# The pooling layer's input product over both column halves at once, and the memory's product in small banks

## The chip, the core and the metric

The kernel runs on one core of a Trainium2 chip. The metric is the device time of one execution in microseconds; three runs of the kernel before are given.

## What is computed

Two decoder layers, on 256 tokens of 1024 features, in float32. Layer 0 matters here:

```python
h = rms_norm(x, g_mix[0]) @ w_in_pool[0]           # 1024 x 1024
tok = pool_mixer(h[..., :768], w_pool_group, pool_scale)   # trailing means - itself, times 4 groups of 192 x 192
qm = h[..., 768:]                                   # 256 columns: 4 heads of 64
mo = mem_cross_attention(qm, rms_norm(mem, g_mem[0]), w_mem_kv[0], ...)   # keys and values: 1024 x 512
x = x + concatenate([tok, mo]) @ w_out[0]
x = x + square(relu(rms_norm(x, g_mlp[0]) @ w_ff1[0])) @ w_ff2[0]
```

Layer 1 has causal attention in place of pooling, the same memory attention with its own weights, and another MLP.

## The kernel before, in words

Every product of float32 matrices is done in three terms. A helper makes two halves of a number: `split` (L105) and `evac_split` (L122) write a high half on the scalar engine (ACT; L113, L125, L128) and a low half on the vector engine (DVE; L114, L126, L129), and `mm3` (L117) issues three matmuls: high by high, high by low, low by high (L118 to L120). Weights come from HBM into slots of `rawp` (7 slots of 512 KB, tag "raw"), all on the queue of the sync engine (SP).

PSUM's eight banks are two pools of four: `accp` for accumulators of products (`accum`, L75) and `psp` for everything that is short (`psum`, L72): transposes, bands, groups, scores.

The input product of layer 0 is x^T (8 chunks of 128 features, two blocks of 128 tokens) by 1024 columns of weights. It runs in two passes over all features: the *B half* (columns 512 to 1023, accumulators `aB`) with loads of x and of the weights in turns (L491 to L512), and then the *A half* (columns 0 to 511, `aA`, L534) by `in_chunk` (L194), which loads two chunks of features in one transfer. Within the A half, hooks issue other work before a given chunk: `queries` before chunk 5 (copies, squares and transposes of the memory's queries, L530), `load_x` before 6 (rows of x for the norms, L526), `load_bands` before 7 (L520).

Then `mix_stats` (L470) forms the norms of x, with a power on POOL (L163); the transposed memory is loaded and split (`mth`, `mtl`); the pooled channels are emptied with the norm (`hhi`, `hlo`). `mem_kv_mm` (L223) makes keys and values of the memory, for layer 0 in `aK` (L616), with the hook `pooling` (L592) before chunk 5: it empties `aA`, loads the group weights, and does four pairs of band products (L563) and three pairs of group products (L580). `mem_kv_norm` and `mem_kv_finish` (L226, L234) read `aK`. The second layer's memory product (`aK1`, L634) follows, with the steps of the memory attention as hooks, and then the output projection, which takes four accumulators.

The program text is not the final order. A planner (the Tile framework's scheduler) gives each engine and each queue a fixed order: among the instructions that its own costs say are ready, the one that stands first in the program goes first. On the chip an engine keeps to that order and waits.

What the change touches, in code:

```python
        hooks = [(PLAN['x'], load_x), (PLAN['q'], queries), (PLAN['bw'], load_bands)]
        aA = in_chunk(xT, w_in_pool[0], 0, GMIX, hooks=hooks)
...
        aK = mem_kv_mm(0, [(PLAN['pool'], pooling)])
```

Of the kernel before, what the change touches and what calls it, by code (L numbers as in the profile page):

```python
# [10 lines left out]
F32 = mybir.dt.float32  # L11
# [7 lines left out]
P = 128  # L19
# [10 lines left out]
# columns of the packed small inputs  # L30
# [6 lines left out]
LAG = 2  # L37
# chunk of features of an input product before which other work is issued (8: after the last), and orders of issue
PLAN = {'x': 6, 'q': 5, 'bw': 7, 'pool': 5, 'mem0': (1, 3, 6, 6),
# [3 lines left out]
B0 = P + 16  # tokens that the first block reaches  # L43

# pairs (input chunk, output chunk) of 128 pooled channels that share a group of 192
# [8 lines left out]
def trunk(ctx: ExitStack, tc: tile.TileContext, x, mem, x_t, mem_t, small, bands, rope, mask,  # L54
# [29 lines left out]
    # the tensor engine's clock rises only under load, and the activation tables load on first use  # L84
# [10 lines left out]
    def load_raw(src):  # L95
        """src: rows (k 128) by n columns, k * n = 1024 -> tile [P, k, n]."""
        n = src.shape[1]
        k = src.shape[0] // P
        r = rawp.tile([P, k, n], F32, tag="raw", name=nm("raw"))
        nc.sync.dma_start(r, src.rearrange("(k p) n -> p k n", p=P))  # L100
        return r
# [20 lines left out]
    def evac_split(ps, hi, lo, g=None):  # L122
        """hi + lo = ps (times the per-partition g)."""
# [7 lines left out]
    def transpose4(src, ncol, hi, lo):  # L131
        """src [P tokens, ncol*128] -> hi/lo [P, ncol, 128 tokens]."""
# [12 lines left out]
    def residual_t(b, h, t):  # L145
        """columns of half h of block b of the residual -> transposed halves."""
# [3 lines left out]
    def norm_stats(src, name, after=None):  # L150
        """mean(src^2) + EPS over the row, [P, 1]."""
# [29 lines left out]
    def head_r(z, nh, eps64, name, ss=None):  # L181
        """(sum(z^2) + 64 eps ms)^-1/2 per head: 1/8 of the head's normalising factor."""
# [11 lines left out]
    def in_chunk(t, w, c0, gcol, c1=None, hooks=()):  # L194
        """token-major (t^T @ (g w)) for 512 columns from c0 on (or 256 from c0 and 256 from c1) -> two accumulators."""
        a = [accum(), accum()]
# [24 lines left out]
    mkp = ctx.enter_context(tc.tile_pool(name="mkp", bufs=1))  # L221

    def mem_kv_mm(l, hooks=()):  # L223
        return in_chunk(memT, w_mem_kv[l], 0, GMEM + 8 * l, hooks=hooks)
# [9 lines left out]
    def mem_kv_finish(l, a, kn, pool):  # L234
        """the normalised keys, transposed, and the values; the last of three steps returns them."""
# [16 lines left out]
    def mem_q(a, b, qT):  # L252
        """queries [P tokens, 256] in PSUM -> transposed hi/lo, and the sums of squares per head."""
# [10 lines left out]
    # work that follows a batch of scores is issued LAG batches later  # L264
# [11 lines left out]
    def exp_t(pool, entries, p, nbuf, put):  # L276
        """entries: (src, n, scale, nbias); later: transposed probabilities [keys, 128] side by side to put()."""
# [27 lines left out]
    def mem_scores(b, j, mq, mk, a, pool, nbuf, put):  # L305
        """heads j, j + 2 of block b -> p^T [keys, (head, key block) 128 tokens]."""
# [14 lines left out]
    def av_out(cat, c0, srcs):  # L321
        """srcs[h][b]: lists of (p^T, values) of 4 heads -> chunks c0, c0 + 1 of the transposed concatenation."""
# [11 lines left out]
    def mem_heads(cat, mq, mk, a, pool, nbuf):  # L334
        """the steps of the memory attention: the scores of either block, then what gathers them."""
# [130 lines left out]
    # ================= layer 0: pooling mixer =================  # L466
# [9 lines left out]
    with tc.tile_pool(name="l0", bufs=1) as lp:  # L476
# [3 lines left out]
        def split_t(src, k, t):  # L480
            """two chunks of 128 features of a transposed input -> its halves."""
            evac_split(src, t[0][:, k:k + 2, :], t[1][:, k:k + 2, :])
# [6 lines left out]
        # first chunk: the loads of x and of the weights take turns  # L489
        aB = [accum(), accum()]  # L490
        for k in range(0, NKC, 2):  # L491
            if k == 0:
                xt = rawp.tile([P, 2, S], F32, tag="raw", name=nm("raw"))
                raws = []
                for j in range(2):
                    nc.sync.dma_start(xt[:, j, :], x_t[:, j, :])
                    raws.append(load_raw(w_in_pool[0][j * P:(j + 1) * P, 512:1024])[:, 0, :])
                    if j == 0:
                        nc.sync.dma_start(sm[:, :16], small[:, :16])
                    evac_split(xt[:, j, :], xT[0][:, j, :], xT[1][:, j, :])  # L500
            else:
                xt = load_t(x_t, k)
                r = load_raw(w_in_pool[0][k * P:(k + 2) * P, 512:1024])
                raws = [r[:, 0, :], r[:, 1, :]]
                if k == 4:
                    nc.sync.dma_start(sm[:, 16:], small[:, 16:])
                split_t(xt, k, xT)
            for j in range(2):
                p = split(raws[j], sm[:, GMIX + k + j:GMIX + k + j + 1])
                for b in range(2):  # L510
                    mm3(aB[b], blk(xT, b, k + j), p, k + j == 0, k + j == NKC - 1)
# [20 lines left out]

        hooks = [(PLAN['x'], load_x), (PLAN['q'], queries), (PLAN['bw'], load_bands)]
        aA = in_chunk(xT, w_in_pool[0], 0, GMIX, hooks=hooks)  # L534
        after_chunk(hooks)
# [3 lines left out]
        # memory: transposed halves  # L539
# [3 lines left out]
        # pooled channels: token-major halves, trailing means, group products  # L543
# [9 lines left out]
        def band(o, w, n, c):  # L553
            """o[128 channels of chunk c, n windows from w on, 256 tokens]: trailing mean minus the value itself."""
# [302 lines left out]
```

## Time and profile before

| | us |
|---|---|
| median of three runs | 572.84 |
| lowest, highest | 572.65, 574.88 |
| span of the profiled execution | 572.7 |
| TensorE (PE) busy | 563.7 |
| DVE busy | 375.6 |
| ACT busy | 340.9 |
| POOL busy | 24.4 |

The span runs from the first to the last instruction of one profiled execution; its own time is not listed beside it, and the three runs are other executions. Busy times of PE are those of a pipelined engine: a matmul of 512 columns shows 0.39 us, but the next starts 0.23 us later. PEld is the load of the stationary operand. "SPq" is the issue of a transfer on the sync engine's queue. A bracket at the end of a timeline row is the idle time of the engine before it, and what ended it.

### The profile page before, as it was taken

How to read it: one execution, taken by the hardware profiler on the slowest of the kernel's cores; microseconds unless marked ns; L12 is line 12 of the kernel's file. 1: busy time of each engine (PE TensorE's matmuls, PEld its weight loads, DVE VectorE, ACT ScalarE, POOL GpSimd, SP SyncE). 2: the span in 40 equal slices, each digit the busy share in tenths (PEclk: the TensorE clock that was granted, in tenths of full speed). 3: DMA queues.
4: the chain of work that ended last, by engine and by line, in shares of the span. 5: the costliest groups of instructions: out<-in, count | busy, mean ns of one | idle time of the engine just before them, and what ended most of it. 6: DMA issues, size and time to landing. Idle time of an engine off the chain costs nothing.

```text
span 572.7 us, 9233 instructions
## 1 busy us (share of the span) xinstructions
PE 563.7 (98%) x3396; PEld 487.0 (85%) x3396; DVE 375.6 (66%) x737; ACT 340.9 (60%) x635; POOL 24.4 (4%) x27
## 2 busy tenths in 40 slices
PE   7999999999999999999999999999999999999997
PEld 3888778989899898898877777889998988989985
DVE  4798977673764754746879999667647457466342
ACT  5789976563663753745766887657536547356230
POOL 0101210000000000000012112000000000000000
PEclk8999999999999999999999999999999999999999
DMA  7988764644836637448473343454466374484201
GB/s 260 338 287 312 236 191 142 200 157 159 260 122 207 222 117 250 167 132 271 144 216 116 111 137 115 124 176 148 145 225 207 123 259 143 152 264 132 84 0 73
DMA packets 46700, 102.00 MB, mean 178 GB/s; under 512 B 3648, under 2 KB 11584, under 8 KB 46656
## 3 DMA queue, kind: packets, MB, share of 16 engines
q1 hardware_dynamic: 46656, 101.43, 55.1%
q8 instruction: 26, 0.43, 0.3%
q14 instruction: 18, 0.15, 0.1%
HBM read 100.37 MB, written 1.05 MB: 177 GB/s over the span
## 4 chain that ended last, share of the span: by engine, by line
PE 91%; DVE 3%; ACT 2%; DMA 1%; POOL 1%; issue 1%; SPq 0%; DVEq 0%; ACTq 0%
PE acc L119 19%; PE acc L118 19%; PE acc L120 19%; PE step L120 9%; PE step L119 9%; PE step L118 9%; PE av_out L331 1%; DMA raw<-in_w_in_pool_dram 1%; PE exp_t L295 1%; POOL r L163 1%; PE transpose L137 1%; PE tok_scores L707 1%; ACT hi L113 1%; DVE lo L114 1%; PE qk_evac L694 1%
## 5 line engine op out<-in xcount | busy, mean ns | idle before, releaser
L114 DVE SCALAR_TENSOR_TENSOR lo<-raw,sm,hi 128x512 fp32r<-128x512 f32 x212 | 149.8, 748 | 43.1 <-ACT hi L113 42.9
L113 ACT ACTIVATE hi<-raw,sm 128x512 fp32r<-128x512 f32 x212 | 142.0, 716 | 56.5 <-PE acc L120 30.2
L111 DVE TENSOR_TENSOR lo<-raw,hi 128x512 fp32r<-128x512 f32 (+1 forms) x152 | 99.5, 687 | 38.7 <-ACT hi L110 38.3
L110 ACT ACTIVATE hi<-raw 128x512 fp32r<-128x512 f32 (+1 forms) x152 | 91.4, 626 | 52.5 <-PE acc L120 42.5
L120 PE MATMUL acc<-hi,hl 128*128 128x512 f32 x256 | 101.1, 395 | 0.0
L118 PE MATMUL acc<-hi,hh 128*128 128x512 f32 x256 | 101.0, 395 | 0.0
L119 PE MATMUL acc<-lo,hh 128*128 128x512 f32 x256 | 101.0, 395 | 0.0
L119 PE MATMUL step<-x1T,hi 128*128 128x256 f32 x224 | 63.4, 283 | 0.0
L120 PE MATMUL step<-x1T,lo 128*128 128x256 f32 x224 | 63.4, 283 | 0.0
L119 PE MATMUL step<-x3T,hi 128*128 128x256 f32 x224 | 63.4, 283 | 0.0
L120 PE MATMUL step<-x3T,lo 128*128 128x256 f32 x224 | 63.4, 283 | 0.0
L118 PE MATMUL step<-x1T,hi 128*128 128x256 f32 x224 | 63.4, 283 | 0.0
L118 PE MATMUL step<-x3T,hi 128*128 128x256 f32 x224 | 63.4, 283 | 0.0
L397 DVE SCALAR_TENSOR_TENSOR h<-step,r 128x512 f32<-128x512 f32 x28 | 19.3, 689 | 67.1 <-ACT r L394 67.1
L120 PEld LDWEIGHTS acc<-hi,hl 128*128 128x128 f32 x256 | 48.2, 188 | 11.2
L394 ACT ACTIVATE r<-step 128x512 f32<-128x512 f32 x28 | 16.5, 588 | 69.1 <-PE step L120 69.1
L118 PEld LDWEIGHTS acc<-hi,hh 128*128 128x128 f32 x256 | 48.3, 189 | 10.5
L119 PEld LDWEIGHTS acc<-lo,hh 128*128 128x128 f32 x256 | 48.2, 188 | 10.5
L118 PEld LDWEIGHTS step<-x3T,hi 128*128 128x128 f32 x224 | 43.0, 192 | 0.3
L118 PEld LDWEIGHTS step<-x1T,hi 128*128 128x128 f32 x224 | 43.0, 192 | 0.3
L119 PEld LDWEIGHTS step<-x3T,hi 128*128 128x128 f32 x224 | 43.0, 192 | 0.3
L119 PEld LDWEIGHTS step<-x1T,hi 128*128 128x128 f32 x224 | 43.0, 192 | 0.3
(155 smaller groups left out, 948.1 us busy)
## 6 DMA issues: line engine op xcount, KB each, us to landing
raw<-in_w_ff_dram SPq DMA_DIRECT2D x128, 512.0 KB, 4.6
raw<-in_w_out_dram SPq DMA_DIRECT2D x16, 512.0 KB, 4.2
raw<-in_w_in_moba_dram SPq DMA_DIRECT2D x24, 256.0 KB, 4.0
raw<-in_w_mem_kv_dram SPq DMA_DIRECT2D x8, 512.0 KB, 5.3
raw<-in_w_in_moba_dram SPq DMA_DIRECT2D x8, 512.0 KB, 4.6
raw<-in_w_in_pool_dram SPq DMA_DIRECT2D x7, 512.0 KB, 7.2
xr<-in_x_dram SPq DMA_DIRECT2D x2, 512.0 KB, 8.5
raw<-in_mem_t_dram SPq DMA_DIRECT2D x4, 256.0 KB, 6.9
```

The source lines that it names most:

```text
L110: nc.scalar.activation(hi, raw, AF.Copy)
L111: nc.vector.tensor_tensor(lo, raw, hi.bitcast(F32), op=ALU.subtract)
L113: last_hi[0] = nc.scalar.activation(hi, raw, AF.Copy, scale=g)
L114: nc.vector.scalar_tensor_tensor(lo, raw, g, hi.bitcast(F32), op0=ALU.mult, op1=ALU.subtract)
L118: nc.tensor.matmul(o, a[0], b[0], start=start, stop=False)
L119: nc.tensor.matmul(o, a[0], b[1], start=False, stop=False)
L120: nc.tensor.matmul(o, a[1], b[0], start=False, stop=stop)
L137: nc.tensor.transpose(ps[:, c * P:(c + 1) * P], src[:, (c0 + c) * P:(c0 + c + 1) * P], ident)
L163: nc.gpsimd.tensor_tensor(r, src, mhalf[:, :n], op=ALU.pow)
L295: nc.tensor.transpose(ps[:, c * P:(c + 1) * P], p[:, c * P:(c + 1) * P], ident)
L394: nc.scalar.activation(r[:, :n], z, AF.Relu)
L397: nc.vector.scalar_tensor_tensor(h[:, :n], z, 0.0, r[:, :n], op0=ALU.max, op1=ALU.mult)
```

## The change

The pooling layer's input product runs once over the features. For each of the 8 chunks one transfer brings all 1024 columns of weights (rows of 4 KB); the first two chunks' halves come in separate transfers of 256 KB, the B halves first. The first weights and the first gains are issued from ACT's queue. The B half of chunk k is multiplied as it comes, the A half of chunk k - 2 after it (`LAG_A = 2`). All four accumulators are taken at once. `load_x`, `queries` and `load_bands` stand after the loop, between the last A pieces. The memory's product of layer 0 accumulates in two banks of the small pool; that of layer 1 still in accumulators. Three entries of `PLAN` and the comments go.

```diff
-PLAN = {'x': 6, 'q': 5, 'bw': 7, 'pool': 5, 'mem0': (1, 3, 6, 6),
+LAG_A = 2
+PLAN = {'pool': 5, 'mem0': (1, 3, 6, 6),
...
-    def in_chunk(t, w, c0, gcol, c1=None, hooks=()):
-        a = [accum(), accum()]
+    def in_chunk(t, w, c0, gcol, c1=None, hooks=(), a=None):
+        a = [accum(), accum()] if a is None else a
...
-    def mem_kv_mm(l, hooks=()):
-        return in_chunk(memT, w_mem_kv[l], 0, GMEM + 8 * l, hooks=hooks)
+    def mem_kv_mm(l, hooks=(), a=None):
+        return in_chunk(memT, w_mem_kv[l], 0, GMEM + 8 * l, hooks=hooks, a=a)
...
-        aB = [accum(), accum()]
-        for k in range(0, NKC, 2):
-            if k == 0:
+        aB, aA = [accum(), accum()], [accum(), accum()]
+        wraw = {}
+
+        def fetch(k):
+            w = w_in_pool[0]
+            if k < 2:
                 xt = rawp.tile([P, 2, S], F32, tag="raw", name=nm("raw"))
-                raws = []
+                nc.sync.dma_start(xt[:, 0, :], x_t[:, k, :])
+                r = rawp.tile([P, 2, 512], F32, tag="raw", name=nm("raw"))
+                q = nc.scalar if k == 0 else nc.sync
+                q.dma_start(r[:, 1, :], w[k * P:(k + 1) * P, 512:1024])
+                if k == 0:
+                    nc.scalar.dma_start(sm[:, :16], small[:, :16])
+                evac_split(xt[:, 0, :], xT[0][:, k, :], xT[1][:, k, :])
+            else:
+                if k % 2 == 0:
+                    xt = load_t(x_t, k)
+                    split_t(xt, k, xT)
+                r = rawp.tile([P, 2, 512], F32, tag="raw", name=nm("raw"))
+                nc.sync.dma_start(r, w[k * P:(k + 1) * P, :].rearrange("p (h n) -> p h n", h=2))
+            wraw[k] = r
+
+        def half(a, k, h):
+            p = split(wraw[k][:, h, :], sm[:, GMIX + k:GMIX + k + 1])
+            for b in range(2):
+                mm3(a[b], blk(xT, b, k), p, k == 0, k == NKC - 1)
+
+        for k in range(NKC):
+            fetch(k)
+            if k == 1:
                 for j in range(2):
-                    nc.sync.dma_start(xt[:, j, :], x_t[:, j, :])
-                    raws.append(load_raw(w_in_pool[0][j * P:(j + 1) * P, 512:1024])[:, 0, :])
-                    if j == 0:
-                        nc.sync.dma_start(sm[:, :16], small[:, :16])
-                    evac_split(xt[:, j, :], xT[0][:, j, :], xT[1][:, j, :])
-            else:
-                xt = load_t(x_t, k)
-                r = load_raw(w_in_pool[0][k * P:(k + 2) * P, 512:1024])
-                raws = [r[:, 0, :], r[:, 1, :]]
-                if k == 4:
-                    nc.sync.dma_start(sm[:, 16:], small[:, 16:])
-                split_t(xt, k, xT)
-            for j in range(2):
-                p = split(raws[j], sm[:, GMIX + k + j:GMIX + k + j + 1])
-                for b in range(2):
-                    mm3(aB[b], blk(xT, b, k + j), p, k + j == 0, k + j == NKC - 1)
+                    nc.sync.dma_start(wraw[j][:, 0, :], w_in_pool[0][j * P:(j + 1) * P, :512])
+            if k == 2:
+                nc.sync.dma_start(sm[:, 16:], small[:, 16:])
+            half(aB, k, 1)
+            if k >= LAG_A:
+                half(aA, k - LAG_A, 0)
...
-        hooks = [(PLAN['x'], load_x), (PLAN['q'], queries), (PLAN['bw'], load_bands)]
-        aA = in_chunk(xT, w_in_pool[0], 0, GMIX, hooks=hooks)
-        after_chunk(hooks)
+        load_x()
+        half(aA, NKC - 2, 0)
+        queries()
+        half(aA, NKC - 1, 0)
+        load_bands()
...
-        aK = mem_kv_mm(0, [(PLAN['pool'], pooling)])
+        aK = mem_kv_mm(0, [(PLAN['pool'], pooling)], [psum("kv"), psum("kv")])
```

## Rows read from the trace of the kernel before

**Rows 1.** The page: the span in 40 slices, the granted TensorE clock in tenths.
```profile
PEclk8999999999999999999999999999999999999999
```

**Rows 2.** Stretches: length, busy us (instructions) per engine, PEclk, DMA share, GB/s.
```profile
0.00:5.00 5.00, 3.48 (x8) 1.03 (x8) 0.77 (x3) 2.48 (x4) 1.11 (x7) 1.00 0.49 149
...
10.00:15.00 5.00, 4.04 (x10) 2.93 (x11) 4.06 (x9) 3.85 (x7) 0.00 (x0) 0.66 1.05 386
15.00:20.00 5.00, 5.00 (x23) 4.12 (x23) 4.14 (x7) 3.88 (x6) 0.00 (x0) 1.00 1.05 394
...
35.00:40.00 5.00, 5.00 (x22) 4.06 (x22) 5.00 (x9) 4.65 (x10) 0.00 (x0) 1.00 0.63 211
```

**Rows 3.** The chain that ended last, 10 to 16 us: start, us, what.
```profile
12.96 0.43 PE acc L119
...
15.91 0.23 PE acc L119
```

**Rows 4.** Timeline of TensorE: first matmuls, a gap, the product's end, the memory's start.
```profile
5.19 0.72 PE L118 MATMUL acc<-hi,xT 128*128 128x512 f32 x2 [0.49 <-ACT hi L113]
...
10.96 0.96 PE L118 MATMUL acc<-hi,xT 128*128 128x512 f32 x2 [1.70 <-ACT hi L113]
...
32.11 0.39 PE L120 MATMUL acc<-hi,xT 128*128 128x512 f32 x1
...
33.93 0.69 PE L118 MATMUL acc<-hi,mth 128*128 128x512 f32 x2
```

**Rows 5.** Timeline of ACT in the first 15 us: what waited for transfers.
```profile
6.49 0.72 ACT L113 ACTIVATE hi<-raw,sm 128x512 fp32r<-128x512 f32 x1 [0.95 <-DMA raw<-in_w_in_pool_dram]
...
8.64 0.63 ACT L125 ACTIVATE xT<-raw 128x512 fp32r<-128x512 f32 x1 [1.43 <-DMA raw<-in_x_t_dram]
...
10.19 1.33 ACT L113 ACTIVATE hi<-raw,sm 128x512 fp32r<-128x512 f32 x2 [0.91 <-DMA raw<-in_w_in_pool_dram]
...
14.87 4.03 ACT L113 ACTIVATE hi<-raw,sm 128x512 fp32r<-128x512 f32 x6 [0.77 <-DMA raw<-in_w_in_pool_dram]
```

**Rows 6.** Timeline of ACT, 20 to 34 us: queries, a split, a norm, memory's weights.
```profile
20.48 0.38 ACT L255 ACTIVATE mq<-acc 128x256 f32<-128x256 f32 x1 [1.59 <-PE acc L120]
...
21.03 0.72 ACT L113 ACTIVATE hi<-raw,sm 128x512 fp32r<-128x512 f32 x1
...
24.01 1.06 ACT L156 ACTIVATE junk<-xr 128x1024 bf16<-128x1024 f32 x1
...
33.12 1.32 ACT L113 ACTIVATE hi<-raw,sm 128x512 fp32r<-128x512 f32 x2
```

**Rows 7.** Two more stretches; a tile's instructions (ns min/median/max); DVE's first split.
```profile
25.05:33.90 8.85, 8.75 (x43) 7.00 (x42) 7.25 (x18) 6.78 (x16) 3.14 (x4) 1.00 0.89 280
23.95:33.10 9.15, 9.05 (x43) 7.20 (x42) 7.53 (x19) 7.08 (x15) 3.14 (x4) 1.00 0.89 289
...
L178 DVE TENSOR_REDUCE ss<-sq x2: 414/418/421, 21.2 to 22.5; 128x4 f32<-128x256 f32 x2
...
33.93 1.41 DVE L114 SCALAR_TENSOR_TENSOR lo<-raw,sm,hi 128x512 fp32r<-128x512 f32 x2
```

**Rows 8.** Timeline: an issue on SP's queue.
```profile
1.18 0.42 SPq L100 DMA_DIRECT2D raw<-in_w_in_pool_dram  x1
```

**Rows 9.** The chain, 43 to 77 us, and TensorE's timeline of the bands.
```profile
43.41 0.61 ACT d L125
44.05 0.69 DVE d L126
...
76.67 0.50 ACT pT L300
...
41.43 0.22 PE L560 MATMUL band<-bw,hhi 128*128 128x128 f32 x1
```

**Rows 10.** Timeline of TensorE and ACT: the waits for the keys, the values' end.
```profile
56.60 0.44 PE L244 MATMUL mem_kv_finish<-ident,kn 128*128 128x128 f32 x2 [0.35 <-DVE kn L231]
...
59.69 0.47 ACT L242 ACTIVATE mv<-acc,r 128x256 f32<-128x256 f32 x1 [0.80 <-DVE kn L231]
```

## The prediction

> **What bounds the kernel now.** The page first: TensorE is busy for 563.7 of 572.7 us, and the clock line has its only reduced slice at the start [rows 1]. So what matters is where TensorE does less than it could. The table of stretches answers that [rows 2]: from 15 to 20 us it is busy in full; before that it is not, and from 10 to 15 us the granted clock averages 0.66. The same table shows why: the DMA engines are half used in the first 5 us (149 GB/s), and full with 386 to 394 GB/s after 10 us.
>
> How much is lost? A dense matmul of 512 columns costs 0.23 us in the chain of waits [rows 3], so a *piece* (one 128-feature chunk, one half of the columns, two blocks, three terms: 6 matmuls) costs 1.37 us with 0.2275 us each, and the product's 16 pieces 21.9 us. It starts at 5.19 and its last matmul ends at 32.5 [rows 4], after 27.3 us, with 0.4 us of transposes in between. So 5.0 us are lost. The scalar engine's waits say what was late [rows 5]: the second weight chunk at 6.49, the second x pair at 8.64, the second weight pair at 10.19. From 9.26 to 10.96 TensorE has nothing [rows 4], and then its clock falls to the lower level of 1.2 GHz: the chain of waits has matmuls 0.43 us apart until 14.7, eight of them, 0.2 us each too long, or 1.6 us [rows 3].
>
> Behind the product the other engines take over. From 43.3 to 77.2 us the chain of waits runs mostly over evacuations, splits and POOL's powers, not over matmuls (the first two and the last of its 85 pieces stand in [rows 9]), and just before, DVE is busy 5.00 of 5 us [rows 2]. So what reaches the end is not when TensorE finishes the product, but when ACT and DVE can start on the memory's weights, now at 33.12 and 33.93 [rows 6, 7].
>
> **The change, part by part.** *The order of the product.* No matmul and no split is added: 96 and 16, as before. Where one half ran through all features before the other began, the A half's pieces now follow two chunks behind the B half's. Per chunk of features 0.66 MB arrive (1.7 us at 390 GB/s [rows 2]), and feed two pieces, 2.7 us of TensorE; before, 0.39 MB fed one piece. Arrivals by bytes: before, the second x pair ended 1.06 MB of requests and was used at 8.64; the second weight pair ended 1.58 MB, at 10.19; the fourth 3.24 MB, at 14.87 [rows 5], so 0.355 MB per us between. After, chunk 0's A half ends 1.06 MB and chunk 2 ends 2.1 MB: 8.64 and 10.19 + 0.52 / 0.355 = 11.65, less 0.4 for the part below, are 8.2 and 11.25. A split's high half takes 0.72 us before TensorE can start, so pieces B0 and B1 run at 4.8 and 7.0, A0 and A1 from 9.0 to 11.9, and from 12.0 the remaining 12 pieces run densely: 12 x 1.37 + 0.4 of transposes gives 28.8 against 32.5, 3.7 us earlier. The clock should then hold, since A0 and A1 stand where the idle time stood.
>
> *Two loads on the scalar queue.* The first weights (256 KB) and 8 KB of gains leave SP's queue, where an issue takes 0.42 us [rows 8]; the first weights no longer stand behind x chunk 0, one issue, and x chunk 1 and weight chunk 1 move up by two, 0.84 us. ACT issues both before its table load, when it has nothing else to do, so nothing waits behind them. I take one issue, 0.4 us, between 0 and 0.84. The DMA engines were half idle then, so a larger gain could be argued. The Trainium skill, "Trainium Kernel Development and Optimization", section Key Constraints, says that issuing from several engines only saves issue time, because all queues run on the same 16 DMA engines; by that, the gain is 0.4 to 0.84 and no more, and no run here yet shows two queues.
>
> *Transfers of all columns.* Rows of 4 KB in place of 2 KB, one DMA more in all (10 for 9). No gain is taken: the stretch at 394 GB/s is nearly all 2 KB rows. What follows on SP's queue keeps its order (x rows, bands, memory), and the same 5.3 MB lie ahead of it, so it lands when it did. A raw slot is held until both halves are split; with 7 slots, I expect no gap, because the splits run ahead of TensorE. If that cover goes, an issue waits one split, 0.7 us.
>
> *What is late next.* The queries and B's pooled channels were emptied beside the A half (from 20.48 on [rows 6]), which now has three pieces behind it. B7 should end three pieces ahead of A7, at 28.8 - 0.4 - 4.1 = 24.3. What DVE must do from there to its first split of the memory's weights is its busy time from 25.05 to 33.90, 7.25 us, and two reductions of 0.42 [rows 7]: 8.1 us. The first block of B7 is done 0.7 us before the second, and the bands' casts need no B7, so it can begin near 23.9: 32.0, 1.9 us before 33.93. ACT: 7.08 us busy from 23.95 to 33.10 [rows 7], less two norms of 1.06 [rows 6], which come before B7 ends, plus two copies and two squares of the queries at 0.38, 1.5: 6.5 us from 24.1 on, 30.6, 2.5 before 33.12. DVE is last, so I take 1.9 of TensorE's 3.7. The bounds: 3.7 if TensorE's time decides, 0 if ACT's queue has the queries ahead of the memory's splits and stands still for B7.
>
> *Small banks.* The memory's first product takes two of the four small banks from its first matmul until its values are read (now at 60.2 [rows 10]); bands and groups have two left. Nothing like it is in the trace. Nearest rows: emptying a band takes 0.61 on ACT and 0.69 on DVE [rows 9], 1.3 us; 7 fillings, of which five would wait for one two before. Between nothing (the memory's matmuls fill in, as between 33.9 and 41.4 [rows 4, 9]) and 5 x 1.3 = 6.5. The banks' cover is 48 matmuls, 11 us, against about 10 us of bands and groups, so near nothing: 0.4. A gain is excluded at this place: the accumulators it took were those of the B half, emptied before A's, and it began at 33.93 behind other work [rows 4]. The second memory product keeps its own banks. The waits for the keys at 56.6 and 59.7 (0.35 and 0.80) [rows 10] are left as they are; they could go or double, 1.1 us each way.
>
> **Sum.** The span of the profiled execution, 572.7, and the median of the three runs, 572.84, are 0.1 apart, so the time around the span is nothing that matters; 572.84 - 1.9 + 0.4 = 571.3 us. After 100 us the work is dense matmuls whose inputs come ahead, so a shift there reaches the end.
>
> **The rivals.** *TensorE decides (faster):* the whole 3.7 us is kept, if the planner puts the memory's splits ahead of the queries' and the bands fill TensorE from 29 us. For it: TensorE is busy in full from 35 to 40 us as well [rows 2]. Against: DVE's 5.00 of 5 us there. 572.84 - 3.7 = 569.1; with the waits for the keys gone, 568.0.
>
> *The banks bind (slower):* the queue order puts bands and groups in a row, and TensorE waits for their evacuation. It decides from four exposed waits: 4 x 1.3 - 1.9 = +3.3, 576.1. For it: at 41.4 to 43.6 four pairs did run in a row [rows 9]. Against: the planner interleaved them with the memory's matmuls at 33.9. The Trainium skill's "TensorE: Matmul & The Clock Gate", section on PSUM-queue depth-cycling, reports that small pauses of TensorE while it cycles through banks can bring the lower clock; no row here shows that, and at the price of the one drop seen, 1.6, it would make this 577.7.
>
> *The start doesn't change (same):* TensorE's fixed order is the program's, B2 ahead of A0, and B2's data come later than before. Then it idles from 8.4 to 12.0, the clock falls again, and 14 pieces, 1.6 and 0.4 follow: 33.2, 0.7 later than 32.5. 572.84 + 0.7 = 573.5. Against: the planner moves work that is ready ahead, as the queries' copy at 20.48 ahead of chunk 4's A split at 21.03, which the program puts before it [rows 6].
>
> **How the numbers follow.** Forecast (about 1.5 faster) 0.36, TensorE decides 0.35, the banks 0.16, start unchanged 0.13. A measurement of this kernel can tell 0.5%, 2.9 us, from no change: below 570.0 is faster, over 575.7 slower. The two rivals that lie beyond these bounds make the outer chances, the other two cases the middle: faster 0.35, same 0.49, slower 0.16. The range takes in the forecast, the unchanged start and nearly all of the faster rival, and ends just inside the banks: 568.0 to 575.6. The cases in the middle have it to themselves from 570.0 to 574.0.
>
> **What would show it.** Right: A pieces between 8.9 and 12 us, granted clock 1.0 throughout after the start; the product's last matmul near 28.8; ACT's first split of the memory's weights near 31 and DVE's near 32; chain still over ACT and DVE at 42 to 75, 1.5 us earlier. Wrong: a lower clock at 10 to 15 us or about 29 us; long waits of a band's or group's matmul for a low half; SP waiting for a raw slot before 20 us.

## The result, and the profile after

The changed kernel takes 579.38 us (577.85 to 580.35, four runs), the kernel before 573.74 beside it: ratio 1.0099, interval 1.0079 to 1.0118. It is slower by 5.6 us, where 571.3 was forecast and 575.6 was the upper end.

One thing about the base: of 77 runs of the kernel before that stand beside the experiments, 46 took 572.3 to 573.5 us with a mean clock of 0.998 to 1.0 and 31 took 573.9 to 575.0, all but two of these with 0.995 to 0.997 (one more run, of 785.43 us at a clock of 0.655, and one of *dense*, of 918.06 us at 0.558, are left out). A run whose span is the profiled execution's 572.7 is listed at 574.4 to 574.5. So kernels are compared by the ratio to the kernel before, run beside them, and the lowest run is given beside the median. Where the intervals of two ratios overlap, a difference between their medians is not clear of noise.

The page's clock line of the changed kernel, as [rows 1]:

```profile
PEclk9998999999999999999999999999999999999999
```

Its stretches, with the columns of [rows 2] and two more for the time behind the product:

```profile
5.00:10.00 5.00, 3.43 (x8) 2.02 (x8) 2.21 (x7) 2.90 (x5) 0.56 (x1) 1.00 0.93 320
10.00:15.00 5.00, 3.23 (x12) 2.01 (x12) 2.73 (x5) 3.21 (x6) 0.00 (x0) 1.00 1.02 381
15.00:20.00 5.00, 5.00 (x24) 4.11 (x23) 4.77 (x8) 3.79 (x7) 0.00 (x0) 1.00 0.79 262
...
45.00:50.00 5.00, 3.46 (x11) 2.84 (x11) 4.59 (x8) 4.86 (x10) 0.00 (x0) 0.69 1.01 382
50.00:55.00 5.00, 5.00 (x38) 4.73 (x38) 3.81 (x7) 4.07 (x8) 0.00 (x0) 0.97 0.72 233
```

The reduced slice has moved from the start to about 45 us. There TensorE is busy 3.46 of 5 us, and the clock averages 0.69 and then 0.97: (0.31 + 0.03) x 5 / 0.5 = 3.4 us at the lower level, which costs half of that, 1.7 us.

TensorE's timeline at the places of [rows 4]:

```profile
6.07 1.22 PE L119 MATMUL acc<-hi,xT 128*128 128x512 f32 x2 [1.26 <-ACT hi L114]
7.09 0.63 PE L120 MATMUL acc<-lo,xT 128*128 128x512 f32 x1
7.52 0.63 PE L121 MATMUL acc<-hi,xT 128*128 128x512 f32 x1
...
13.20 1.11 PE L119 MATMUL acc<-hi,xT 128*128 128x512 f32 x3 [1.72 <-ACT hi L114]
...
32.82 0.40 PE L121 MATMUL acc<-hi,xT 128*128 128x512 f32 x1
33.05 0.40 PE L119 MATMUL kv<-hi,mth 128*128 128x512 f32 x1
```

The first piece is 0.9 us later than before, its matmuls stand 0.43 us apart (the spacing of 1.2 GHz in [rows 3], though the stretch's column says 1.00), and TensorE is idle again before 13.20. The product's last matmul is 0.7 us later than before, not 3.7 earlier. Yet the memory's product begins 0.9 earlier. Most of the loss lies behind it. The MLP's first matmul, in the changed kernel and then in the kernel before:

```profile
102.55 0.28 PE L119 MATMUL acc<-x1T,hi 128*128 128x256 f32 x1
```

```profile
97.47 0.28 PE L118 MATMUL acc<-x1T,hi 128*128 128x256 f32 x1
```

These are 5.1 us, and from there the difference stays (the spans are 577.7 and 572.7).

What TensorE waited for up to 110 us (us in total, times, longest), first in the changed kernel, then in the kernel before:

```profile
PE acc L119 <- ACT hi L114: 3.5, 3, 1.7
PE band L576 <- DVE d L127: 1.5, 1, 1.5
...
PE exp_t L296 <- DVE s L290: 0.8, 1, 0.8
PE mem_kv_finish L245 <- DVE sst L186: 0.7, 1, 0.7
PE mem_kv_finish L245 <- DVE kn L232: 0.7, 1, 0.7
PE kv L120 <- DVE lo L115: 0.2, 1, 0.2
```

```profile
PE acc L118 <- ACT hi L113: 2.2, 2, 1.7
...
PE mem_kv_finish L244 <- DVE kn L231: 1.2, 2, 0.8
```

So the account of the 5.1 us is: 0.7 at the product's end, 1.5 for a band, 1.7 for the clock that falls behind that wait, 0.8 for the probabilities (exp_t), 0.2 for the keys (0.7 + 0.7 against 1.2), 0.2 for the memory's first low half (kv): 5.1. The 0.7 flatters the change, since the clock had fallen in this execution of the kernel before [rows 2]; in *before_pool4* below, the same kernel up to there, it held, and the product's last matmul stands at 30.45. The band's wait is a chain over three engines. ACT, DVE and TensorE around it, in the changed kernel:

```profile
44.52 0.72 ACT L114 ACTIVATE hi<-raw,sm 128x512 fp32r<-128x512 f32 x1 [1.54 <-DMA raw<-in_w_mem_kv_dram]
45.27 0.38 ACT L126 ACTIVATE d<-band 64x256 fp32r<-64x256 f32 x1
...
46.06 0.43 DVE L127 TENSOR_TENSOR d<-band,d 64x256 fp32r<-64x256 f32 x1
...
46.64 0.54 PE L576 MATMUL band<-bw,hhi 128*128 128x512 f32 x1 [1.53 <-DVE d L127]
```

The second half of a band lies finished in its bank, but in ACT's fixed order its emptying stands behind a split of the memory's weights, and that split waits 1.54 us for a transfer. The bank comes free when DVE has written its half too, at 46.5. The bands are late as a whole: ACT empties the A half's pooled channels, from which they are made, behind the first splits of the memory's weights and no longer ahead of them. ACT in the changed kernel, then in the kernel before, where those splits begin at 33.12 [rows 6]:

```profile
31.85 1.35 ACT L114 ACTIVATE hi<-raw,sm 128x512 fp32r<-128x512 f32 x2
...
35.45 1.29 ACT L129 ACTIVATE hhi<-acc,r 128x512 fp32r<-128x512 f32 x2
```

```profile
31.86 1.37 ACT L128 ACTIVATE hhi<-acc,r 128x512 fp32r<-128x512 f32 x2 [0.57 <-PE acc L120]
```

The start has a cause of its own. The issues on SP's queue, first of the changed kernel, then of the kernel before, and the first weights' issue on ACT's queue in the changed one:

```profile
1.18 0.41 SPq L523 DMA_DIRECT2D raw<-in_w_in_pool_dram  x1
1.65 0.42 SPq L525 DMA_DIRECT2D sm<-in_small_dram  x1
2.11 0.43 SPq L545 DMA_DIRECT2D xr<-in_x_dram  x1
2.59 0.43 SPq L499 DMA_DIRECT2D raw<-in_x_t_dram  x1
3.06 0.43 SPq L502 DMA_DIRECT2D raw<-in_w_in_pool_dram  x1
```

```profile
2.11 0.43 SPq L496 DMA_DIRECT2D raw<-in_x_t_dram  x1
2.59 0.43 SPq L100 DMA_DIRECT2D raw<-in_w_in_pool_dram  x1
```

```profile
1.23 0.39 ACTq L502 DMA_DIRECT2D raw<-in_w_in_pool_dram  x1
```

With two loads gone from SP, the planner filled the place: A weights of chunk 0 (256 KB, L523), 85 KB of gains and 512 KB of x rows, all of which the program has behind x chunk 1, now stand ahead of x chunk 1 (2.59, was 2.11) and chunk 1's weights (3.06, was 2.59). The first weights, on ACT's queue behind the gains, left at 1.23, where SP had sent them at 1.18 [rows 8]. So of what TensorE waits for at the start only the 8 KB of gains were issued sooner than before, at 0.73.

### The profile page after: what moved, and what is told of

It is laid out like the page before. It is cut to its first block, busy times and chain, and to the rows that moved or that the text cites. A ratio compares the mean times of both kernels' runs of the same rounds, so it can differ in the third digit from the quotient of the medians.

```text
span 577.7 us, 9241 instructions
## 1 busy us (share of the span) xinstructions
PE 565.1 (98%) x3396; PEld 487.9 (84%) x3396; DVE 375.4 (65%) x737; ACT 341.9 (59%) x635; POOL 24.3 (4%) x27
## 4 chain that ended last, share of the span: by engine, by line
PE 89%; DVE 4%; DMA 3%; ACT 1%; POOL 1%; issue 1%; SPq 0%; DVEq 0%; ACTq 0%
PE acc L119 18%; PE acc L121 18%; PE acc L120 18%; PE step L121 9%; PE step L120 9%; PE step L119 9%; DMA raw<-in_w_in_pool_dram 2%; DVE lo L115 2%; PE av_out L332 2%; PE exp_t L296 1%; POOL r L164 1%; PE transpose L138 1%; PE tok_scores L726 1%; DMA raw<-in_w_mem_kv_dram 1%; PE qk_evac L713 1%
## 5 line engine op out<-in xcount | busy, mean ns | idle before, releaser
L115 DVE SCALAR_TENSOR_TENSOR lo<-raw,sm,hi 128x512 fp32r<-128x512 f32 x212 | 149.6, 746 | 44.4 <-ACT hi L114 44.3
```

Of the source, the lines that this page charges most:

```text
L115: nc.vector.scalar_tensor_tensor(lo, raw, g, hi.bitcast(F32), op0=ALU.mult, op1=ALU.subtract)
```

## The experiments

All with the median, the lowest run, and the ratio to the kernel before, run beside them (0.001 of it is 0.57 us):

| run | from | median | lowest | ratio, interval |
|---|---|---|---|---|
| after | | 579.38 | 577.85 | 1.0099 [1.0079, 1.0118] |
| spq | after | 577.91 | 576.34 | 1.0083 [1.0054, 1.0113] |
| acc | after | 579.19 | 577.84 | 1.0090 [1.0063, 1.0117] |
| spq_acc | after | 578.77 | 577.24 | 1.0085 [1.0051, 1.0119] |
| before_small | before | 575.76 | 574.81 | 1.0040 [1.0024, 1.0056] |
| lag1 | spq_acc | 576.72 | 575.54 | 1.0059 [1.0038, 1.0080] |
| ramp | spq_acc | 576.12 | 575.22 | 1.0046 [1.0029, 1.0063] |
| pool4 | spq_acc | 577.00 | 575.41 | 1.0073 [1.0048, 1.0098] |
| before_late_q | before | 574.64 | 572.91 | 1.0014 [1.0000, 1.0029] |
| held | after | 576.36 | 575.73 | 1.0048 [1.0033, 1.0063] |
| lag1_pool4 | lag1 | 575.22 | 574.53 | 1.0031 [1.0015, 1.0046] |
| dense | ramp | 573.67 | 573.16 | 1.0003 [0.9991, 1.0014] |
| dense_pool4 | dense | 573.20 | 572.44 | 0.9990 [0.9980, 1.0000] |
| dense_banks | dense_pool4 | 576.54 | 575.64 | 1.0054 [1.0037, 1.0071] |
| dense_queue | dense_pool4 | 572.13 | 571.43 | 0.9983 [0.9970, 0.9995] |
| before_pool4 | before | 574.38 | 573.88 | 1.0029 [1.0017, 1.0041] |

### Undo the queue, the banks, both

*spq* puts the two loads back on SP:

```diff
-                q = nc.scalar if k == 0 else nc.sync
+                q = nc.sync
...
-                    nc.scalar.dma_start(sm[:, :16], small[:, :16])
+                    nc.sync.dma_start(sm[:, :16], small[:, :16])
```

> The changed kernel with the first weights and the first gains on SP's queue, as before. Three theories. START: with the two loads on ACT's queue the planner put 85 KB of gains and 512 KB of x rows ahead of x chunk 1 on SP's queue, and that is what made the product end 4 us later than forecast; here x rows come after all weights again, the first matmul is at about 5.2 us in place of 6.1 and the product ends near 29.5 in place of 33.2. If START carries to the end: about 3 us less, 576.4. BANKS: the 1.5 us wait of a band for a bank and the half clock behind it (1.7 us) are the cost, they stay wherever the product ends, and the time stays within 1 us of 579.4. ORDER: chunk 2's B piece stands ahead of chunk 0's A piece in TensorE's order, so the gap before it remains and the product ends near 32: 578.

*acc* gives the memory's product its accumulators back, and *spq_acc* does both:

```diff
-        aK = mem_kv_mm(0, [(PLAN['pool'], pooling)], [psum("kv"), psum("kv")])
+        aK = mem_kv_mm(0, [(PLAN['pool'], pooling)])
```

> The changed kernel with the memory's first product in accumulators, as before; four small banks for bands and groups. BANKS: no wait of a band for a bank, the clock stays at its upper level after the start, 3.2 us less: 576.2. START: the start is untouched, product's end stays near 33.2, and the time within 1 us of 579.4, because other work takes the place of the wait. If both are partly right, 577 to 578.

> Both edits together: only the order of the product's halves and the full-width transfers are left of the change. START and BANKS adding up: 3 and 3.2 us less than the changed kernel, 573.2, or level with the kernel before. ORDER: the product's start is no better than before, and the time lands 0 to 2 us over the kernel before. If the halves together are worth what was forecast: 571 to 572.

The queue gives back 1.5 us in both columns (by the ratios 0.9, with intervals that overlap), the banks nothing that can be told, and both together no more. In *spq* the first matmul comes at 5.36, and the product's last at 31.76 instead of 32.82. In *acc* the band's wait is gone and another stands in its place; ACT and TensorE of *acc*:

```profile
44.30 0.72 ACT L114 ACTIVATE hi<-raw,sm 128x512 fp32r<-128x512 f32 x1 [2.08 <-DMA raw<-in_w_mem_kv_dram]
45.04 1.00 ACT L126 ACTIVATE d<-band 64x256 fp32r<-64x256 f32 x2
...
45.47 0.39 PE L119 MATMUL group<-d,hi 128*128 128x256 f32 x1 [1.72 <-ACT d L126]
```

ACT stands at the same transfer, now for 2.08 us, and with the banks free it is the first group that waits for the band's half. What binds is ACT's order behind a transfer that lands late, and the bank only named the instruction that showed it.

### The banks alone, in the kernel before

```diff
-        aK = mem_kv_mm(0, [(PLAN['pool'], pooling)])
+        aK = mem_kv_mm(0, [(PLAN['pool'], pooling)], [psum("kv"), psum("kv")])
```

(`mem_kv_mm` and `in_chunk` take the accumulators as an argument, as in the change.)

> The kernel before with the one edit that the memory's first product accumulates in two small banks. BANKS: a band waits for a bank for 1 to 1.5 us and the clock may fall after it: 575 to 577 against 573.7. START: banks alone cost nothing here, since the bands begin before the memory's product: 573 to 574.

It is 2.9 us slower by the medians, 2.3 by the ratio (1.0040). TensorE of this kernel at the product's end:

```profile
30.21 0.39 PE L120 MATMUL acc<-hi,xT 128*128 128x512 f32 x1
31.98 0.73 PE L118 MATMUL kv<-hi,mth 128*128 128x512 f32 x2 [1.39 <-ACT hi L113]
```

Before, band products began at 32.60, right behind the product, and covered the time until the memory's first split. With two banks held by the memory's product, the planner's order has that product's first matmuls ahead of the bands, and TensorE waits 1.39 us. The keys' wait has grown by 0.5 us (1.7 against 1.2); the rest of the cost is not placed.

### The order of the pieces, the plan, and the emptying

*lag1* is *spq_acc* with A one chunk behind B (and the last pieces in a loop that follows it); *ramp* lets the lag grow, so that B7 stands four pieces ahead of A7:

```diff
-LAG_A = 2
+LAG_A = 1
```

```diff
-LAG_A = 2
+AFTER = {1: 0, 2: 1, 4: 2, 6: 3}
...
-            if k >= LAG_A:
-                half(aA, k - LAG_A, 0)
+            if k in AFTER:
+                half(aA, AFTER[k], 0)
```

> The changed kernel with both loads back on SP's queue and the memory's product in the accumulators (578.77 us), and now the A half's pieces one chunk behind the B half's instead of two, so that TensorE's order has A0 ahead of B2. Theory ORDER (TensorE idles from 10.6 to 12.1 us because B2 stands ahead of A0, whose weights lie in the memory by 8.3): that idle time falls under 0.4 us, the product's last matmul starts near 30.3 instead of 31.7, and the time falls by 1 to 1.5 us, to about 577.5. Theory EMPTYING (what the time follows is when ACT and DVE have emptied the B half, and the memory's and bands' pieces that TensorE has for cover): the start gains the same, but B7 ends only two pieces before A7, so that less of the emptying is covered, and of the 1.4 us at most 0.5 is left at 100 us: 578.3 to 579. Theory MIDDLE (the planner's order of bands and memory pieces, with all bands in a row and groups right behind them, makes the waits at 46.5, 60 to 65 and 75 to 80 us, 3 us in all): the time follows those waits, whatever the start does; with the memory pieces back between bands and groups it comes to 574 to 576.

> As the run with a lag of one chunk, but the lag grows: A0 behind B1, A1 behind B2, A2 behind B4, A3 behind B6, and A4 to A7 behind B7. So the start is that of the lag of one, and the B half ends four pieces (5.5 us) before the A half, as against two or three. Theory ORDER: as with the lag of one, about 577.5. Theory EMPTYING: the queries and the B half's pooled channels are emptied beside TensorE's last four pieces, so ACT and DVE reach the memory's weights 1.5 to 2.5 us sooner than in the run with both undone, and the time is 575 to 576.5, 1.5 or more under the lag of one. Theory MIDDLE: the time follows the waits behind 40 us; no fixed sign against the lag of one.

TensorE in *spq_acc*, where A0 is the third of the matmuls at 12.11, behind two of B2, and then in *lag1*, with the end of its product:

```profile
12.11 1.12 PE L119 MATMUL acc<-hi,xT 128*128 128x512 f32 x3 [1.52 <-ACT hi L114]
```

```profile
10.37 0.40 PE L119 MATMUL acc<-hi,xT 128*128 128x512 f32 x1
...
30.09 0.40 PE L121 MATMUL acc<-hi,xT 128*128 128x512 f32 x1
31.84 0.97 PE L577 MATMUL band<-bw,hhi 128*128 128x256 f32 x4 [1.35 <-ACT hhi L129]
```

A0 could run at 10.37. ORDER holds in the trace: the idle time is gone, and the product's last matmul stands at 30.09 instead of 31.70. The time falls by 2.05 us (by the ratios 1.5, with intervals that overlap). EMPTYING falls for the most part: *ramp*, with four A pieces (5.5 us) behind B7 in place of two, gains only 0.6 against *lag1*, inside both intervals. The other test of it:

```diff
-PLAN = {'x': 6, 'q': 5, 'bw': 7, 'pool': 5, 'mem0': (1, 3, 6, 6),
+PLAN = {'x': 6, 'q': 8, 'bw': 7, 'pool': 5, 'mem0': (1, 3, 6, 6),
```

> The kernel before, whose order, queue, transfers and banks all stay, with one number of its plan changed: the queries are written behind the A half's last chunk (8) instead of ahead of its chunk 5, so that their share of the emptying of the B half lies where the change puts it, behind or beside the end of the pooling product. Theory EMPTYING: the bands start later, since ACT's and DVE's work for the queries now falls into the time from 30 to 40 us; slower than before by 1 to 3 us (574 to 576). Theories ORDER and MIDDLE: the time of the kernel before within 0.6 us, unless the planned order of bands and memory pieces changes.

The lowest runs differ by 0.4 us, the ratio is 1.0014. It is a weak test: the planner still put the queries' copies beside the A half, and only their transposes came later. It leaves open what a truly late emptying costs.

*pool4* changes one number of the plan, behind the product:

```diff
-PLAN = {'pool': 5, 'mem0': (1, 3, 6, 6),
+PLAN = {'pool': 4, 'mem0': (1, 3, 6, 6),
```

> The changed kernel with both loads back on SP's queue and the memory's product in the accumulators (578.77 us), with the bands and groups written ahead of the memory product's chunk 4 instead of chunk 5; the start and the pooling product are untouched. Theories ORDER and EMPTYING: no change beyond 0.5 us, since the product and its emptying are the same. Theory MIDDLE: the planned order has one memory piece among bands and groups again, so the wait of 0.96 us at the groups falls under 0.3, and the time falls by 0.5 to 1.5 us, to 577.3 to 578.3.

ACT in *pool4*: the bands' halves now leave before the memory's weights are due.

```profile
41.71 1.41 ACT L126 ACTIVATE d<-band 128x512 fp32r<-128x512 f32 x3 [0.72 <-PE band L580]
43.18 0.72 ACT L114 ACTIVATE hi<-raw,sm 128x512 fp32r<-128x512 f32 x1
```

The groups' wait of 0.96 us is gone, and the lowest run falls by 1.8 us, the median by as much; by the ratios it is 0.7, and the intervals overlap, since the six runs lie 4 us apart.

### Hold the hoisted loads back; fill the start; both

*held* is the changed kernel, with the gains tied behind the weights of chunk 2, and the x rows behind the last weights:

```diff
-                nc.sync.dma_start(sm[:, 16:], small[:, 16:])
+                with tc.issue_after(held[0].ins):
+                    nc.sync.dma_start(sm[:, 16:], small[:, 16:])
...
-        load_x()
+        with tc.issue_after(held[0].ins):
+            load_x()
```

> The changed kernel (579.38 us) with its queues, order of pieces and small banks as they are, but the x rows (512 KB) and the 85 KB of gains, which the planner had put on SP's queue ahead of x chunk 1, are tied behind the weights of chunk 2 and the last weights they follow in the program. It tells the second queue itself from what the planner made of it. Theory START: all of what the loads on one queue gave back (1.5 us) comes back here too, because it was the hoisted bytes that held x chunk 1 and its weights up: the clock is full from about 5 us, the first matmul comes near 5.3 instead of 6.07, the time is 577.9 or less. If the second queue itself costs (an issue on ACT late, or two queues sharing the DMA engines), the clock rises only at 9 us as in the changed kernel and the time stays at 579 to 579.5.

It gains 3.0 us, with intervals apart, and so START's claim on the hoist holds. But not its picture of the first matmul: that comes at 7.38, later than ever, because the planner now has the split of x chunk 1 ahead of the first weights' on ACT:

```profile
6.29 0.42 ACT L126 ACTIVATE xT<-raw 128x256 fp32r<-128x256 f32 x1 [2.44 <-DMA raw<-in_x_t_dram]
6.62 1.32 ACT L114 ACTIVATE hi<-raw,sm 128x512 fp32r<-128x512 f32 x2
```

B0 and B1 then run without a gap, but with a clock of 0.87 from 5 to 10 us and 0.79 from 10 to 15, and the product's last matmul is at 31.48. So 1.3 of the 3.0 us stand at the product's end and the rest behind it.

*lag1_pool4* joins two edits; *dense* puts the first three A pieces right behind their B pieces and loads chunk 0's A weights ahead of x chunk 1; *dense_pool4* is both.

```diff
-            if k == 1:
-                for j in range(2):
-                    nc.sync.dma_start(wraw[j][:, 0, :], w_in_pool[0][j * P:(j + 1) * P, :512])
+            if k < 2:
+                nc.sync.dma_start(wraw[k][:, 0, :], w_in_pool[0][k * P:(k + 1) * P, :512])
...
-AFTER = {1: 0, 2: 1, 4: 2, 6: 3}
+AFTER = {0: 0, 1: 1, 2: 2, 4: 3, 6: 4}
```

> Loads on SP's queue, the memory's product in the accumulators, A's pieces one chunk behind B's (576.72 us), and bands and groups written ahead of the memory product's chunk 4. With a lag of two chunks that number of the plan gave 1.8 us (577.00 against 578.77). Theories ORDER and MIDDLE, if what they gave back is separate: 576.72 - 1.8 = 574.9, and what stays against the kernel before is 1.9 us. If the two are the same time seen twice (the lag of one had already put a memory piece back between bands and groups in TensorE's order): 576.2 to 577.

> Loads on SP's queue, the memory's product in the accumulators, and each of the first three chunks' A piece right behind its B piece, with the A weights of chunk 0 loaded ahead of x chunk 1; from chunk 3 on the B half runs ahead, so that B7 ends three pieces before A7. Theory ORDER: the arrivals (0.36 MB per us) now feed TensorE without the idle 1.3 us at 7.3 as well, which every run had so far; the product's last matmul starts near 28.7 us instead of 30.1 to 30.2, and the clock is full; the time is 1.3 us under the run whose lag grows (576.12): 574.8. Theory EMPTYING (the time follows ACT and DVE behind the product, which have as much to do and now less of it done by then): at most 0.4 of the 1.4 us is kept at 100 us, 575.7 or more.

> As the run before in this list, and bands and groups ahead of the memory product's chunk 4. Theories ORDER and MIDDLE together, if separate: 574.8 - 1.8 = 573.0, the kernel before's time. Theory EMPTYING: 575 or more. If it falls under 572 both kernels are beaten.

*dense* gains 2.5 us against *ramp*, with intervals apart. Against *spq_acc*, from which it differs in nothing but the order of the pieces and of the first A loads, it gains 5.1 by the medians, 4.7 by the ratios and 4.1 by the lowest runs, again with intervals apart: this order is most of the loss. The number of the plan comes on top with 1.5 us in *lag1_pool4* and 0.5 in *dense_pool4*, neither clear of the intervals. TensorE at the product's end in *dense_pool4*:

```profile
28.99 0.39 PE L121 MATMUL acc<-hi,xT 128*128 128x512 f32 x1
30.79 0.97 PE L576 MATMUL band<-bw,hhi 128*128 128x256 f32 x4 [1.41 <-ACT hhi L129]
```

This matmul ends at 29.4, where the prediction's sum had 28.8, with 0.4 taken off for a second queue that this kernel lacks. And the time is only that of the kernel before.

### Still open after these: banks, queue and plan, each alone

*dense_banks* and *dense_queue* start from *dense_pool4*; *before_pool4* is the kernel before with 'pool': 4. In *dense_queue* the two loads are the first two instructions on ACT's queue, the table load is tied behind them, and the gains and x rows are held as in *held*:

```diff
+    r0 = rawp.tile([P, 2, 512], F32, tag="raw", name=nm("raw"))
+    w0B = nc.scalar.dma_start(r0[:, 1, :], w_in_pool[0][:P, 512:1024])
+    g0 = nc.scalar.dma_start(sm[:, :16], small[:, :16])
...
-    nc.scalar.activation(touch, mhalf[:, :1], AF.Exp)
+    with tc.issue_after(g0.ins):
+        nc.scalar.activation(touch, mhalf[:, :1], AF.Exp)
```

> The fastest of the kernels so far (dense_pool4, 573.20 us: loads on one queue, A's pieces close behind B's, bands ahead of chunk 4) with the memory's first product back in two of the four small banks. Theory BANKS: bands and groups have two banks again, and nothing now hides that; waits of a band's or group's matmul of 0.5 us and more appear between 30 and 50 us, and the time rises by 1.5 to 3 us, to 574.7 to 576.2, as it did in the kernel before (2.9). If the banks are no cost of their own (as the 0.2 us in the changed kernel say): within 0.5 us of 573.2.

> dense_pool4 (573.20 us) with the first weights and the first 8 KB of gains issued by the scalar engine, ahead of its table load, and the x rows and the other gains tied behind the weights they follow in the program, so that nothing is hoisted on SP's queue. The prediction's step: x chunk 1 and chunk 1's weights are issued up to 0.9 us earlier than at 2.1 and 2.6 us, and 0.4 us (0 to 0.84) reach the first pieces: 572.4 to 573.2. If the DMA engines and not the issues set the arrival (the engines shared by every load in flight), the first matmul stays at 5.2 and the time at 573.2 within 0.4. If the scalar engine's start is late (table load, touch, first x split behind two issues), the first matmul comes 0.3 to 0.9 later and the time is 573.5 to 574.1.

> The kernel before with one number of its plan changed: bands and groups written ahead of the memory product's chunk 4 instead of 5. Theory MIDDLE as a cost of the change (the planned order of before fits its own emptying, and the changed emptying no longer fits it): no gain here, 572.8 to 574. If the number is worth the same everywhere: 571.2 to 572.

TensorE of *dense_banks*, then the first issue on SP's queue and TensorE of *dense_queue*:

```profile
29.74 0.39 PE L121 MATMUL acc<-hi,xT 128*128 128x512 f32 x1
32.73 0.73 PE L119 MATMUL kv<-hi,mth 128*128 128x512 f32 x2 [2.60 <-ACT hi L114]
```

```profile
0.74 0.39 SPq L526 DMA_DIRECT2D raw<-in_w_in_pool_dram  x1
...
5.71 1.12 PE L123 MATMUL acc<-hi,xT 128*128 128x512 f32 x3 [0.90 <-ACT hi L118]
...
28.24 0.39 PE L125 MATMUL acc<-hi,xT 128*128 128x512 f32 x1
```

The banks cost 3.3 us, with intervals apart, and not by waits of bands for each other. The gap of 2.60 is at the same place as in *before_small*, and stands where *dense_pool4* has one of 1.41; besides, the product ends 0.75 later, and the wait for the probabilities is 0.7 longer (0.9 against 0.2). The queue, with the gains and x rows held, gains 1.1 (1.0 by the lowest runs; the intervals of the ratios overlap). Its first matmul is 0.5 later (5.71 against 5.19): the planner now has chunk 0's A weights (0.74) ahead of x chunk 0, which ACT splits at 4.63 instead of 3.28. But then TensorE waits for nothing until the product's end, 0.75 sooner. This is the fastest kernel, 0.17% under the kernel before, interval 0.05 to 0.30%. Moving the bands ahead of chunk 4 costs the kernel before 1.4 us, clear of its interval, where it gave 0.5 to 1.8 by the medians in the changed orders: the number is worth something only beside the order it fits.

## Why the prediction was wrong

None of the four cases gave what came. The highest, the banks with the lower clock, had 577.7 us, and the banks are not what bound. These steps failed:

- **The order of the pieces.** "Pieces B0 and B1 run at 4.8 and 7.0, A0 and A1 from 9.0 to 11.9" is the step that failed first, and the costliest. B0 ran at 6.07, B1 at 9.49, and A0 not before 13.20. The argument was that the planner moves ready work ahead, read from ACT's queue [rows 6]. On TensorE it kept the program's order, A0 behind B2, and the third rival's sum, 33.2 us for the product's end, is what came (32.82 + 0.4). That its number fits is partly luck: it had the clock fall at 10 to 15 us, where the column shows 1.00, and did not have the late first piece. *lag1* shows that the order is the cause of the gap, *dense* that orders of pieces and loads are worth 4.7 of the 5.6 us, and *dense_pool4* that the arithmetic by arrivals was nearly sound: 29.4 for 28.8.
- **What an earlier end is worth.** 1.9 of the 3.7 us were credited, against the median. But 1.6 of the 3.7 were the fallen clock of the profiled execution (32.11 against 30.45 in *before_pool4*), and the median of the three runs, 572.84, lies among those in which the clock doesn't fall. So a loss was to be removed that the base did not have; "572.7 and 572.84 are 0.1 apart" compared a span with a time, and about 1.8 us lie around the span (577.7 and 579.53 in the changed kernel's profiled run). The rest meets a new wait: 1.41 us for the pooled channels in *dense_pool4*. The faster rival, "TensorE decides", is refuted by *dense_pool4*: its product's last matmul stands 1.5 us sooner than that 30.45, and its lowest run, 572.44, is only 0.2 under that of the kernel before beside it.
- **Two loads on the scalar queue.** 0.4 (0 to 0.84) was priced as issues saved on SP. The size is right where little else moves (0.75 at the product's end in *dense_queue*). What failed is "x chunk 1 and weight chunk 1 move up by two": the queue is the planner's to refill, and it hoisted 0.85 MB into the gap (256 KB of A weights, 85 and 512 KB). *held* prices the 0.6 MB of gains and x rows at 3.0 us. The Trainium skill, "Trainium Kernel Development and Optimization", Key Constraints, says that issuing from several engines saves issue time only; the 0.75 us of *dense_queue* agree, being no more than two issues of 0.42.
- **Transfers of all columns.** No gain and no gap were expected, and TensorE shows neither from 15 us on. From 15 to 20 us 262 GB/s were moved against 394 [rows 2], but the wide transfers are not the reason: *dense_pool4* has the same ones and moves 408.
- **What is late next.** DVE and ACT were said to reach the memory's weights early, and they did, in spite of the late product: 31.85 for ACT and 32.80 for DVE, against 33.12 and 33.93. What the step left out is that the A half's pooled channels are then emptied behind these splits, at 35.45, and that the bands, which began at 32.60 before, begin at 40.44, so that their emptying on ACT stands among splits whose weights land at 44.3 to 44.5. That the loss behind the product, 4.4 of 5.1 us, comes of this is argued and not shown: *pool4*, which moves the bands ahead, gives back 1.8, not clear of noise, and *dense* nearly all with the plan left as it is.
- **Small banks.** 0.4, between 0 and 6.5: the cost is 2.9 to 3.3 us where nothing else covers it, between the 0.4 taken and the slower rival's 4 x 1.3 = 5.2. But its mechanism, pairs that wait for the emptying of one two before, appears once, for 1.53 us, in the changed kernel, where *acc* shows that ACT's order had made it; in *before_small* and *dense_banks* the largest part that can be seen is the gap before the memory's first split (1.39, and 1.2 more than in *dense_pool4*). In the changed kernel the banks cost nothing that could be told, since the other waits stand in the same place. "TensorE: Matmul & The Clock Gate" of the Trainium skill, section on PSUM-queue depth-cycling, ties frequent small pauses while TensorE cycles through banks to the lower clock. Here one pause of 1.53 us was followed by 0.69, but *acc*, with one of 1.72 us, kept its clock, so the runs neither bear this out nor refute it.

What stays open: whether the plan's number alone gives the 1.8 us, and how they divide between ACT's order and the transfers that change with it, since *pool4* moves both; how much of what *dense* regains behind the product comes of the earlier end; and what emptying late costs by itself.

## What to carry to other kernels

Where a planner fixes the order, taking an instruction from a queue need not move the next up; here it opened a place that the planner filled with whatever was ready, and a change of order must be written into the program, piece by piece, on the engine that is to follow it. A retuned number of a plan belongs to the order that it was tuned for: after the stage ahead has changed, look at what stands behind a waiting split on ACT before blaming the bank or engine that the wait names. And set the sum against the profiled execution's own time, and ask whether the loss to be removed is in the median at all.

## What the runs showed of the hardware

- The clock doesn't fall behind every pause. It fell in the profiled run of the kernel before, behind 1.70 us of idle time [rows 4], and held in that of *before_pool4*, behind 1.66 us at the same place (1.00 from 10 to 15 us); in *spq_acc* pauses of 1.25 and 1.52 us within 5 us left it at full speed.
- A transfer that is issued first isn't done before later ones begin to move. Chunk 1's B weights, 256 KB, issued at 2.59 us, were used at 6.49 in the kernel before [rows 5] and at 7.82 in *spq_acc*, both times behind a wait for them. The requests up to and with them are 128 + 256 + 8 + 128 + 256 KB, 0.79 MB, in both; moved by then were 153 GB/s x 6.49 us = 0.99 MB and 177 x 7.82 = 1.38 MB, so at least 0.2 and 0.6 MB belong to transfers issued later. In *spq_acc* the next two issues are A weights of 256 KB each, before they were 256 KB of x and 512 KB of weights; why the wait is longer in *spq_acc* is not shown. Its row:

```profile
7.82 0.72 ACT L114 ACTIVATE hi<-raw,sm 128x512 fp32r<-128x512 f32 x1 [1.89 <-DMA raw<-in_w_in_pool_dram]
```
